# Hi and lo weight parts in one pair tile, placed by how many columns move past them

## The chip, the cores and the metric

The kernel runs on one core of one Trainium2 chip. The metric is the device time of one execution in microseconds (us), lower is better. TensorE is called PE in the profile, its weight loads PEld; VectorE is DVE, ScalarE is ACT, GpSimd is POOL, SyncE is SP.

## The reference

Two decoder layers over one sequence of 512 tokens, 2048 wide, in float32. Each layer is an RMSNorm with a shift, scale and gate made from a conditioning vector, then a mixer, then a residual add; a last RMSNorm follows.

```python
for i in range(DEPTH):                                   # DEPTH = 2
    shift, scale, gate = jnp.split((silu(c) @ ada_w[i] + ada_b[i])[:, None, :], 3, axis=-1)
    h = rmsnorm(x, norm_g[i]) * (1.0 + scale) + shift
    y = retention_branch(...) if i == 0 else mla_branch(...)
    x = x + gate * y
return rmsnorm(x, final_norm_g)
```

`retention_branch` projects `h` (2048) to q, k (8 heads of 256 each), v and a gate (8 heads of 512 each), rotates q and k, runs a causal retention with a decay per head, normalises per head, multiplies with SiLU of the gate and projects 4096 back to 2048. `mla_branch` projects `h` to two latents of 512, a rotary key of 64 and a gate of 2048, expands the latents to 16 heads (192 for q and k, 128 for v), runs causal attention, multiplies with SiLU of the gate and projects 2048 back to 2048.

## The kernel before, in words

*Three matmuls for one product.* A float32 operand is split into a hi part, rounded to the type `float32r`, and a lo part, the rest: ACT writes hi with a copy, DVE writes lo with a subtraction (`split`, L136). A product is then three matmuls into one PSUM bank: hi by hi, hi by lo, lo by hi (`mm3`, L161; the same order by hand at L409, L806 to L808, L905, L1387, L1651 and L2309). Each matmul is preceded by a load of its 128 by 128 stationary operand (LDWEIGHTS), and 256 or 512 columns of the other operand then move through.

*Where weights live.* A weight block of 2 x 512 columns comes by DMA into a `raw` tile (three of them), and its parts go into a tile of tag `whi` and one of tag `wlo`, 4096 bytes per partition each, three of each. `load_w` (L140) does this for the plain projections, `plain_steps` (L738) for the listed steps, `o1_unit` (L1367), `o2_unit` (L2259), `first_load` (L319) and `unit_prepare` (L1870) for their own. `turns` (L782) hands out tiles in turn for the steps with seven products: three out of four times `whi` and `wlo`, the fourth time a tile pair of the open pool (`own_h`, `own_l` in pool `lp`, two tiles `bm` in `l2`). Some units use tiles of other tags instead (`big`, `k4b`).

*Where 512 columns move, and where 256.* In most stages the weight part is stationary and a whole row of 512 tokens moves, or 128 tokens are stationary and 512 weight columns move. Four places have 256 columns moving past stationary weight parts:

- `seven_rows_steps` (L887, its matmul at L905): the q and k projections of heads 2 to 5 and two of the four gate blocks of the second layer (`g2`). A 2 x 2 block product is made from seven half-size products, so half the tokens, 256, move at a time. Its `prepare` (L931) forms the sums on DVE and splits them.
- `ga_half` (L1639, L1651), the first three units of the second layer's first gate block.
- `tail_block` (L1474, L1387), the last four units of the first layer's output projection.
- `o2_end` (L2322, L2309), the last four units of the second layer's.

*Order.* The work is a list of `Step`s: loads run three units ahead on SP's queue, `prepare` one step ahead on DVE and ACT, `multiply` on PE; `behind` and `queued` fix each engine's order as written. Further DVE work goes beside the steps: products for the modulation (L1089), rotations, softmax.

*Layout.* SBUF tiles lie one behind the other in the order in which their tags first appear, in units of 32 bytes, the base pool first and the pools `l0`, `lp`, `l1` and `l2` in turn behind it. An unused tile `spacer` of 32 bytes (L125) and an oversized `qn_s` (L1743) fill it up. By the sum of the sizes `big` begins at byte 6976 of a partition, the `whi` and `wlo` tiles at 147008 and the open pool at 171840; these and all the tiles of 4096 and 2048 bytes between them start 64 bytes past a multiple of 128 (and of 256).

Of the kernel before, what the change touches and what calls it, by code (L numbers as in the profile page):

```python
# [9 lines left out]
F32 = mybir.dt.float32  # L10
# [39 lines left out]
def hybrid_trunk_kernel(  # L50
# [88 lines left out]

    def load_w(parts, a, b, name, later=None, where=None):  # L140

        raw = base.tile([P, a, b], F32, tag="raw", bufs=3, name=f"{name}_raw")
        for dst, src in parts:
            nc.sync.dma_start(dst(raw), src)
        where = where or (("whi", 3), ("wlo", 3))
        hi, lo = (
            base.tile([P, a, b], F32R, tag=tag, bufs=n, name=f"{name}_{p}") for p, (tag, n) in zip(("hi", "lo"), where)
        )
        if later is None:
            split(raw, hi, lo)  # L150
        else:
            later.append(lambda: split(raw, hi, lo))
        return hi, lo
# [165 lines left out]
    def first_load(kind, u):  # L319

        cn = 512
        tags = (("k4b", 4), ("k4b", 4)) if kind == "g" else (("whi", 3), ("wlo", 3))
        raw = big(f"{kind}0_{u}_raw", F32) if u == 0 else base.tile(
            [P, 2, cn], F32, tag="raw", bufs=3, name=f"{kind}0_{u}_raw"
        )
        c0 = {"v": 4096, "g": 8192}.get(kind)
        for dst, src in qk_parts(0, u) if kind == "qk" else [(whole, rows(w_ret_in, u, 2, c0, cn))]:
            nc.sync.dma_start(dst(raw), src)

        def prepare():  # L330
            hl = [base.tile([P, 2, cn], F32R, tag=t, bufs=n, name=f"{kind}0_{u}_{t}{i}") for i, (t, n) in enumerate(tags)]
# [376 lines left out]
    lp = tc.tile_pool(name="lp", bufs=1)  # L708
    lpp = lp.__enter__()

    def keep_rows(ps, dst_d, r0, name, func=AF.Identity, own=None):
# [25 lines left out]

    def plain_steps(nu, kn, parts, cn, name, take, n, lhs, rhs, evac, seeded=False, **kw):  # L738

        banks = {}  # L740

        def step(u):
# [7 lines left out]
            def prepare():  # L750
                w["hl"] = [
                    base.tile([P, kn, cn], F32R, tag=tag, bufs=3, name=f"{name}_{u}_{tag[1]}") for tag in ("whi", "wlo")
                ]
                split(w["raw"], *w["hl"])
# [26 lines left out]

    def turns(raw_tags, part_tags):  # L782
# [8 lines left out]
        def part_tiles(shape, name):  # L791
            n[1] += 1
            pool, tags, bufs = part_tags[n[1] % len(part_tags)]
            return [pool().tile(shape, F32R, tag=tag, bufs=bufs, name=f"{name}_{p}") for p, tag in zip("hl", tags)]

        return raw_tile, part_tiles

    def seven_steps(h, block, form, raw_tile, part_tiles, finish, rows):


        x_, s_, y_, z_, m1, m4, m5 = ([None] * 2 for _ in range(7))
# [13 lines left out]
        def step(second, u):  # L815
# [14 lines left out]
            def prepare():  # L830
                e, o = w["e"], w["o"]
                if not second:
                    eh, el = part_tiles([P, 2, T], f"{n}e")
                    DVE.tensor_sub(e[:, 1, :], e[:, 1, :], e[:, 0, :])
# [3 lines left out]
                    DVE.tensor_sub(el, e, eh.bitcast(F32))  # L838
                    oh, ol = part_tiles([P, 2, T], f"{n}o")
                    ACT.copy(oh, o)  # L840
# [3 lines left out]
                else:  # L844
                    oh, ol = part_tiles([P, 2, T], f"{n}o")
# [3 lines left out]
                    eh, el = part_tiles([P, T], f"{n}e")  # L849
                    ACT.copy(eh, e)  # L850
# [36 lines left out]
    def seven_rows_steps(name, load_half, acts, sums, raw_tile, part_tiles, finish, rows):  # L887
# [30 lines left out]
        def step(second, u):  # L918
# [12 lines left out]
            def prepare():  # L931
                e, o = w["e"], w["o"]
                if not second:
                    e0, e1, o0, o1 = (t[:, :, j * H : (j + 1) * H] for t in (e, o) for j in range(2))
                    eh, el = part_tiles([P, 2, T], f"{n}e")
                    DVE.tensor_sub(e1, e1, e0)
# [3 lines left out]
                    DVE.tensor_sub(el, e, eh.bitcast(F32))  # L940
                    oh, ol = part_tiles([P, 2, T], f"{n}o")
                    ACT.copy(oh, o)
# [3 lines left out]
                else:  # L946
                    oh, ol = part_tiles([P, 2, T], f"{n}o")
# [4 lines left out]
                    eh, el = part_tiles([P, T], f"{n}e")  # L952
                    ACT.copy(eh, e)
# [35 lines left out]
    def heads_steps(h):  # L989
# [24 lines left out]
        ((lambda: lpp, "own_r", 3), (lambda: base, "raw", 3)),  # L1014
        ((lambda: lpp, ("own_h", "own_l"), 1), *3 * ((lambda: base, ("whi", "wlo"), 3),)),
    )
# [141 lines left out]
    def retention(h, own, own2=None):  # L1158
# [207 lines left out]

    def o1_unit(n, r, u, kn, cn, where=(("whi", 3), ("wlo", 3))):  # L1367
# [12 lines left out]
        return w, (load, prepare)  # L1380
# [72 lines left out]
    def second_out():  # L1453
        outs(2, range(4))
        for b in range(4):
# [5 lines left out]
            3, 0, u, 1, 2 * T,  # L1461
            {4: 2 * (("big", 16),), 5: 2 * (("big", 16),), 6: 2 * (("k4b", 4),)}.get(u, (("whi", 3), ("wlo", 3))),
        )
# [155 lines left out]
    rotary2, kr = [], {}  # L1619

    def l2_tile(tag, bufs, name, shape=(P, T), dt=F32):
        return pools["l2"].tile(list(shape), dt, tag=tag, bufs=bufs, name=name)
# [13 lines left out]

    ga = g2_steps(0, seeded=True)

# [103 lines left out]

    qn_s = base.tile([P, 32], F32, name="qn_s")[:, :NT]  # L1743

# [24 lines left out]
    def latent_parts(n, g_c):  # L1769
# [9 lines left out]

    wc = w_mla_in[:, 0:1024].rearrange("k (j n) -> k j n", j=2)  # L1780
    turns2 = turns(
        ((lambda: pools["l2"], "bw", 2), (lambda: base, "raw", 3)),
        ((lambda: pools["l2"], ("bm", "bm"), 2), *3 * ((lambda: base, ("whi", "wlo"), 3),)),
    )
    steps += seven_steps(
# [84 lines left out]
    def unit_prepare(kind, pr, u):  # L1870
        raw = unit_raw.pop((kind, pr, u))
        cn, tags = (384, (("whi", 3), ("wlo", 3))) if kind == "uq" else (512, 2 * (("k4b", 4),))
        hi, lo = unit_parts[kind, pr, u] = [
            base.tile([P, 2, cn], F32R, tag=t, bufs=n, name=f"{kind}_{pr}_{u}_{i}") for i, (t, n) in enumerate(tags)
        ]
        if kind == "ukv":
# [69 lines left out]
    def attend(h):  # L1946
# [13 lines left out]
        def exps(i):  # L1960
            n = (i + 1) * P
            if i == 0:
                side["sm"] = small(f"sm_{h}", NT)
                if s == 0:
                    p_.extend(l2_tile("pp", 5, f"p_{h}_{j}") for j in range(NT))
                else:
                    both = [l2_tile("bm", 2, f"p_{h}_{j}", (P, 2, T)) for j in range(2)]
                    p_.extend(both[j // 2][:, j % 2, :] for j in range(NT))
            DVE.tensor_add(ps[i][:, i * P : n], ps[i][:, i * P : n], mask)
# [187 lines left out]
    for i, step in enumerate(steps):  # L2157
        if i == n_p:
            lp.__exit__(None, None, None)
            l1 = tc.tile_pool(name="l1", bufs=1)  # L2160
            pools["l1"] = l1.__enter__()
        if i == n_l2:
            l1.__exit__(None, None, None)
            l2 = tc.tile_pool(name="l2", bufs=1)
            pools["l2"] = l2.__enter__()
        with behind(S_):
            while n_loaded < min(n_prepared + 3, len(loads)):
# [305 lines left out]
```

## Time and profile before

| | us |
|---|---|
| median of 3 runs | 2149.7 (2149.39 to 2150.03) |
| the profiled execution, its own time | 2149.59 |
| span of that execution, first to last instruction | 2147.8 |
| PE busy in it | 2122.6 |
| DVE busy | 1675.3 |
| ACT busy | 1056.7 |

The granted TensorE clock was 0.998 over the span. "L905" is line 905 of the kernel before. A matmul's recorded duration overlaps with the next one's, so the time that a matmul takes is read from start to start, or from the length of a stretch and the number of matmuls in it.

### The profile page before, as it was taken

What the parts mean: (1) busy time and instruction counts of PE and PEld (TensorE: products, weight loads), DVE (VectorE), ACT (ScalarE), POOL (GpSimd) and SP (SyncE); (2) the same over time, 40 slices, a digit from 0 to 9 for tenths busy, and PEclk for the clock granted to TensorE, in tenths of its full rate; (3) what the DMA queues carried; (4) which work ended last, traced back from release to release, by engine and by line L of the source; (5) the groups of instructions that cost most, each with busy time, mean ns of one, the idle gap of its engine ahead of it and who ended that gap; (6) DMA issues with size and microseconds to landing.
All of it is one profiled execution on the core that took longest, in us unless ns stands there. A gap on an engine that the chain in (4) does not pass through costs nothing.

```text
span 2147.8 us, 30042 instructions
## 1 busy us (share of the span) xinstructions
PE 2122.6 (99%) x11100; PEld 1824.9 (85%) x11100; DVE 1675.3 (78%) x2482; ACT 1056.7 (49%) x1604; POOL 106.5 (5%) x178
## 2 busy tenths in 40 slices
PE   7999999999999999999999999999999999999998
PEld 5887898988889888888888888898889989988887
DVE  7899788888878789766777777668978788886745
ACT  5764444444444444434344544445446565664434
POOL 1000000000000000000000000010001000000000
PEclk9999999999999999999999999999999999999999
DMA  9976687877777778755647566553456644346734
GB/s 381 395 281 197 225 277 229 275 241 259 255 259 259 237 235 283 261 181 185 237 155 246 185 207 240 169 176 115 159 189 203 187 128 147 118 133 221 244 109 137
DMA packets 229782, 462.96 MB, mean 216 GB/s; under 512 B 20817, under 2 KB 84337, under 8 KB 225793
## 3 DMA queue, kind: packets, MB, share of 16 engines
q1 hardware_dynamic: 217424, 421.85, 59.6%
q0 software_dynamic: 11920, 38.91, 4.6%
q8 instruction: 87, 1.43, 0.3%
q14 instruction: 61, 0.50, 0.1%
q10 hardware_dynamic: 290, 0.27, 0.0%
HBM read 417.96 MB, written 43.00 MB: 215 GB/s over the span
## 4 chain that ended last, share of the span: by engine, by line
PE 82%; DVE 7%; DMA 5%; issue 2%; ACT 2%; POOL 1%; SPq 0%; DVEq 0%; POOLq 0%; ACTq 0%
PE o L1387 9%; PE o L2309 4%; PE x L806 2%; PE x L807 2%; PE y L806 2%; PE s L806 2%; PE x L808 2%; PE y L808 2%; PE s L808 2%; PE s L807 2%; PE y L807 2%; PE y_qk L905 2%; PE s_qk L905 2%; PE x_qk L905 2%; DMA mod<-in_ada_t_dram 2%
## 5 line engine op out<-in xcount | busy, mean ns | idle before, releaser
L1387 PE MATMUL o<-o_h,o_whi 128*128 128x512 f32 (+1 forms) x496 | 192.3, 388 | 0.0
L1387 PE MATMUL o<-o_h,o_wlo 128*128 128x512 f32 (+1 forms) x496 | 191.9, 387 | 0.1
L1387 PE MATMUL o<-o_l,o_whi 128*128 128x512 f32 (+1 forms) x496 | 191.3, 386 | 0.0
L1387 PEld LDWEIGHTS o<-o_h,o_wlo 128*128 128x128 f32 x496 | 93.2, 188 | 20.1 <-DVE o_wlo L138 1.5
L138 DVE TENSOR_TENSOR o_wlo<-o_r,o_whi 128x1024 fp32r<-128x1024 f32 x61 | 74.5, 1223 | 44.1 <-ACT o_whi L137 43.5
L1387 PEld LDWEIGHTS o<-o_h,o_whi 128*128 128x128 f32 x496 | 93.2, 188 | 18.2
L1387 PEld LDWEIGHTS o<-o_l,o_whi 128*128 128x128 f32 x496 | 93.2, 188 | 18.2
L165 PE MATMUL qk<-hT,qk_l 128*128 128x512 f32 x192 | 74.8, 390 | 1.5 <-DVE qk_l L138 1.5
L358 DVE SCALAR_TENSOR_TENSOR aw<-aw,c_all 128x2048 f32<-128x2048 f32 (+1 forms) x35 | 73.0, 2101 | 2.7 <-DMA aw<-in_ada_t_dram 2.6
L163 PE MATMUL qk<-hT,qk_h 128*128 128x512 f32 x192 | 75.0, 391 | 0.0
L164 PE MATMUL qk<-hT,qk_h 128*128 128x512 f32 x192 | 74.7, 389 | 0.0
L1089 DVE SCALAR_TENSOR_TENSOR mod<-mod,c_odd 128x1024 f32<-128x1024 f32 x48 | 58.0, 1220 | 20.1 <-DMA mod<-in_ada_t_dram 20.1
L137 ACT CAST o_whi<-o_r 128x1024 fp32r<-128x1024 f32 x61 | 63.4, 1051 | 20.8 <-PE o L1387 18.4
L138 DVE TENSOR_TENSOR o_w_lo<-o_w_raw,o_w_hi 128x1024 fp32r<-128x1024 f32 x32 | 38.9, 1220 | 32.7 <-ACT o_w_hi L137 32.6
L1089 DVE SCALAR_TENSOR_TENSOR mod<-mod,c_bm 128x1024 f32<-128x1024 f32 x48 | 58.5, 1219 | 0.0
L2309 PE MATMUL o<-o_h,o_w_hi 128*128 128x512 f32 (+1 forms) x160 | 55.6, 348 | 0.0
L2309 PE MATMUL o<-o_h,o_w_lo 128*128 128x512 f32 (+1 forms) x160 | 55.5, 347 | 0.0
L2309 PE MATMUL o<-o_l,o_w_hi 128*128 128x512 f32 (+1 forms) x160 | 55.4, 347 | 0.0
L1242 ACT ACTIVATE yn<-y,nmr,gn_r 128x512 f32<-128x512 f32 x32 | 22.3, 778 | 62.0 <-DVE nmr L1236 62.0
L137 ACT CAST o_w_hi<-o_w_raw 128x1024 fp32r<-128x1024 f32 x32 | 33.5, 1050 | 36.3 <-PE o L2309 32.5
L164 PE MATMUL o<-o_l,o_w_hi 128*128 128x512 f32 x128 | 50.1, 391 | 0.5 <-DVE o_l L138 0.5
L137 ACT CAST o_h<-o_in 128x1024 fp32r<-128x1024 f32 x24 | 25.2, 1052 | 51.1 <-PE o L164 47.2
(1608 smaller groups left out, 6893.4 us busy)
## 6 DMA issues: line engine op xcount, KB each, us to landing
mod<-in_ada_t_dram SPq DMA_DIRECT2D x96, 512.0 KB, 5.8
o_r<-in_ret_w_out_dram SPq DMA_DIRECT2D x64, 512.0 KB, 5.3
aw<-in_ada_t_dram SPq DMA_DIRECT2D x30, 1024.0 KB, 9.0
mod_gate<-in_ada_t_dram SPq DMA_DIRECT2D x32, 512.0 KB, 5.0
o_w_raw<-in_mla_w_out_dram SPq DMA_DIRECT2D x32, 512.0 KB, 4.0
qk_r<-in_ret_w_in_dram SPq DMA_DIRECT2D x48, 256.0 KB, 3.2
qk_r<-qk_d SPq DMA_DIRECT2D x32, 256.0 KB, 5.7
v_r<-v_d SPq DMA_DIRECT2D x32, 256.0 KB, 6.2
```

Of the source, the lines that this page charges most:

```text
L137: ACT.copy(hi, src)
L138: DVE.tensor_sub(lo, src, hi.bitcast(F32))
L163: PE.matmul(o, lhs[0], rhs[0], start=first and not seeded, stop=False, skip_group_check=seeded)
L164: PE.matmul(o, lhs[0], rhs[1], start=False, stop=False, skip_group_check=seeded)
L165: return PE.matmul(o, lhs[1], rhs[0], start=False, stop=last, skip_group_check=seeded)
L806: PE.matmul(banks[b], a[0], w[0], start=first, stop=False, skip_group_check=True)
L807: PE.matmul(banks[b], a[0], w[1], start=False, stop=False, skip_group_check=True)
L808: PE.matmul(banks[b], a[1], w[0], start=False, stop=True, skip_group_check=True)
L905: PE.matmul(o, w[wp][:, i, b * P : (b + 1) * P], a[ap], start=first and i + b + k == 0, stop=k == 2, skip_group_check=True,)
L1089: DVE.scalar_tensor_tensor(out=aw, in0=aw, scalar=1.0, in1=silu_c[j], op0=ALU.mult, op1=ALU.mult, accum_out=mc[:, j, b : b + 1],)
L1387: PE.matmul(o, w[i][:, ki, c0 + b * P : c0 + (b + 1) * P], a[j], start=first and i + j == 0, stop=last and i == 1, skip_group_check=True,)
L2309: PE.matmul(banks2[b][:, cols], w[0][i][:, 0, b * P : (b + 1) * P], o2_moving(w, u, cols)[j], start=u + i + j == 0, stop=u == KD - 1 and i ...
```

## The change: what it does

The tags `whi` and `wlo` go. In their place stand three tiles `pair0` to `pair2` of 2 x 1024 + 16 float32 each (8256 bytes, which is 64 more than two parts). A hi and a lo part are views of one pair, 1024 elements apart, beginning at element 16 (`EVEN`) or at element 0 (`ASIDE`). `ASIDE` is given at the four places where 256 columns move past stationary weight parts, as far as their parts lie in pairs: all of `seven_rows_steps`, the first three units of `ga`, unit 7 of the first output projection's tail, the last two units of the second's. All else is `EVEN`. The pools' own parts are pairs likewise (`own`).

Further: the pairs are allocated between the small column tiles at the start of the base pool; `rt` and `mhalf` become one tile, `spacer` goes, `qn_s` shrinks to 64 bytes, the tag `st6` of pool `l1` goes (its four tiles come from `small`), and pool `l1` begins with a `gap` of 64 bytes. The probabilities of every second head (`exps`) lie in the own pair of `l2` instead of two `bm` tiles.

```diff
-    mhalf = base.tile([P, NT], F32, name="mhalf")
+    few = base.tile([P, 2 * NT], F32, name="few")
+    rt, mhalf = few[:, :NT], few[:, NT:]
     DVE.memset(mhalf, -0.5)
-    rt = base.tile([P, 4], F32, name="rt")
-    spacer = base.tile([P, 8], F32, name="spacer")
-    DVE.memset(spacer, 0.0)
...
-    def load_w(parts, a, b, name, later=None, where=None):
+    def load_w(parts, a, b, name, later=None, where=None, halved=False):
...
-        where = where or (("whi", 3), ("wlo", 3))
-        hi, lo = (
-            base.tile([P, a, b], F32R, tag=tag, bufs=n, name=f"{name}_{p}") for p, (tag, n) in zip(("hi", "lo"), where)
-        )
+        hi, lo = two_tiles(where, [P, a, b], name, ASIDE if halved else EVEN)
...
-    a_col = [base.tile([P, KD], F32, name=f"a_col{i}") for i in range(2)]
-    b_col = [base.tile([P, KD], F32, name=f"b_col{i}") for i in range(2)]
-    gate_c = [base.tile([P, KD], F32, name=f"gate_c{i}") for i in range(2)]
+    EVEN, ASIDE = 16, 0
+
+    def pair_tile(pool, tag, name):
+        return pool.tile([P, 2 * 1024 + EVEN], F32R, tag=tag, bufs=1, name=name)
+
+    a_col, b_col, gate_c, ready, n_pairs = [], [], [], {}, [0]
+    for i in range(3):
+        ready[i] = pair_tile(base, f"pair{i}", f"pair_{i}")
+        if i < 2:
+            for cols, name in ((a_col, "a_col"), (b_col, "b_col"), (gate_c, "gate_c")):
+                cols.append(base.tile([P, KD], F32, name=f"{name}{i}"))
+
+    def next_pair(name):
+        i = n_pairs[0] % 3
+        n_pairs[0] += 1
+        return ready.pop(i, None) or pair_tile(base, f"pair{i}", name)
+
+    def parts_of(pair, shape, at):
+
+        n = math.prod(shape[1:])
+        views = [pair[:, 1024 * i + at : 1024 * i + at + n] for i in range(2)]
+        return views if len(shape) == 2 else [v.rearrange("p (k n) -> p k n", k=shape[1]) for v in views]
+
+    def two_tiles(where, shape, name, at=EVEN):
+
+        if where is None:
+            return parts_of(next_pair(name), shape, at)
+        return [base.tile(list(shape), F32R, tag=t, bufs=n, name=f"{name}_{i}") for i, (t, n) in enumerate(where)]
...
     def seven_rows_steps(...)
...
-                    eh, el = part_tiles([P, 2, T], f"{n}e")
+                    eh, el = part_tiles([P, 2, T], f"{n}e", ASIDE)
...
-                st = l1_tile("st6", 4, f"st_{h}_{i}", (P, 6))
+                st = small(f"st_{h}_{i}", 6)
...
-            hl = [base.tile([P, kn, cn], F32R, tag=t, bufs=b, name=f"o1_{n}_{r}_{u}_{t}{i}") for i, (t, b) in enumerate(where)]
+            hl = two_tiles(where, [P, kn, cn], f"o1_{n}_{r}_{u}_p", ASIDE if kn == 1 and u > 3 else EVEN)
...
-    ga = g2_steps(0, seeded=True)
+    ga = g2_steps(0, seeded=True, halved=3)
...
-    qn_s = base.tile([P, 32], F32, name="qn_s")[:, :NT]
+    qn_s = base.tile([P, 16], F32, name="qn_s")[:, :NT]
...
+            l1_tile("gap", 1, "gap", (P, EVEN))
...
-        wt = load_w([(whole, rows(w_mla_out, u, kn, r * T, cn))], kn, cn, f"o2_w{r}_{u}", where=where)
+        halved = kn == 1 and u >= KD - 4
+        wt = load_w([(whole, rows(w_mla_out, u, kn, r * T, cn))], kn, cn, f"o2_w{r}_{u}", where=where, halved=halved)
```

More of the change, by code (lines that the diff above doesn't have):

```diff
@@ L321, in first_load @@
         cn = 512
-        tags = (("k4b", 4), ("k4b", 4)) if kind == "g" else (("whi", 3), ("wlo", 3))
+        where = (("k4b", 4), ("k4b", 4)) if kind == "g" else None
         raw = big(f"{kind}0_{u}_raw", F32) if u == 0 else base.tile(
@@ L330, in prepare @@
         def prepare():
-            hl = [base.tile([P, 2, cn], F32R, tag=t, bufs=n, name=f"{kind}0_{u}_{t}{i}") for i, (t, n) in enumerate(tags)]
+            hl = two_tiles(where, [P, 2, cn], f"{kind}0_{u}_p")
             ACT.copy(hl[0], raw)
@@ L750, in prepare @@
             def prepare():
-                w["hl"] = [
-                    base.tile([P, kn, cn], F32R, tag=tag, bufs=3, name=f"{name}_{u}_{tag[1]}") for tag in ("whi", "wlo")
-                ]
+                w["hl"] = two_tiles(None, [P, kn, cn], f"{name}_{u}_p", ASIDE if u < halved else EVEN)
                 split(w["raw"], *w["hl"])
@@ L780, in halves, with turns @@
         return tuple((t[0][:, j, :], t[1][:, j, :]) for j in range(n))
-    def turns(raw_tags, part_tags):
+    def turns(raw_tags, own):
         n = [0, 0]
@@ L789, in raw_tile, with part_tiles @@
             return pool().tile(shape, F32, tag=tag, bufs=bufs, name=f"{name}_r")
-        def part_tiles(shape, name):
+        def part_tiles(shape, name, at):
             n[1] += 1
-            pool, tags, bufs = part_tags[n[1] % len(part_tags)]
-            return [pool().tile(shape, F32R, tag=tag, bufs=bufs, name=f"{name}_{p}") for p, tag in zip("hl", tags)]
+            return parts_of(next_pair(name) if n[1] % 4 else own(name), shape, at)
         return raw_tile, part_tiles
     def seven_steps(h, block, form, raw_tile, part_tiles, finish, rows):
+        at = EVEN
         x_, s_, y_, z_, m1, m4, m5 = ([None] * 2 for _ in range(7))
@@ L1014, in hybrid_trunk_kernel @@
         ((lambda: lpp, "own_r", 3), (lambda: base, "raw", 3)),
-        ((lambda: lpp, ("own_h", "own_l"), 1), *3 * ((lambda: base, ("whi", "wlo"), 3),)),
+        lambda name: own_ready.pop() if own_ready else pair_tile(lpp, "own", name),
     )
@@ L1619, in hybrid_trunk_kernel, with l2_pair @@
     rotary2, kr = [], {}
+    l2_ready = []
+    def l2_pair(name):
+        return l2_ready.pop() if l2_ready else pair_tile(pools["l2"], "own", name)
     def l2_tile(tag, bufs, name, shape=(P, T), dt=F32):
@@ L1780, in hybrid_trunk_kernel @@
     wc = w_mla_in[:, 0:1024].rearrange("k (j n) -> k j n", j=2)
[L1781 to L1784, printed above, removed]
+    turns2 = turns(((lambda: pools["l2"], "bw", 2), (lambda: base, "raw", 3)), lambda name: l2_pair(name))
     steps += seven_steps(
@@ L1871, in unit_prepare @@
         raw = unit_raw.pop((kind, pr, u))
[L1872 to L1875, printed above, removed]
+        cn, where = (384, None) if kind == "uq" else (512, 2 * (("k4b", 4),))
+        hi, lo = unit_parts[kind, pr, u] = two_tiles(where, [P, 2, cn], f"{kind}_{pr}_{u}_p")
         if kind == "ukv":
@@ L1966, in exps @@
                 else:
-                    both = [l2_tile("bm", 2, f"p_{h}_{j}", (P, 2, T)) for j in range(2)]
-                    p_.extend(both[j // 2][:, j % 2, :] for j in range(NT))
+                    both = l2_pair(f"p_{h}_").bitcast(F32)
+                    p_.extend(both[:, j * T : (j + 1) * T] for j in range(NT))
             DVE.tensor_add(ps[i][:, i * P : n], ps[i][:, i * P : n], mask)
```

22 lines of the change are left out of this document (12 added, 10 removed).

## The prediction

> **What bounds the kernel now.** I read the page first: its busy table, and the shares of the chain of work that ended last.
>
> ```profile
> span 2147.8 us, 30042 instructions
> ...
> PE 2122.6 (99%) x11100; PEld 1824.9 (85%) x11100; DVE 1675.3 (78%) x2482; ACT 1056.7 (49%) x1604; POOL 106.5 (5%) x178
> ...
> PE 82%; DVE 7%; DMA 5%; issue 2%; ACT 2%; POOL 1%; SPq 0%; DVEq 0%; POOLq 0%; ACTq 0%
> ```
>
> PE is busy all the time and carries 82% of the chain, so what counts is how often a matmul starts. PE's busy time can't tell that: a matmul's recorded duration overlaps the next one's. So the second view is the table of busy times by stretch, for stretches that hold one shape alone. Columns: stretch, its length, busy time and instruction count of PE, PEld, DVE, ACT and POOL, granted clock, DMA share, GB/s.
>
> ```profile
> 323.41:399.60 76.19, 76.19 (x339) 63.07 (x337) 63.21 (x79) 35.52 (x42) 3.59 (x7) 1.00 0.75 242
> 283.10:323.41 40.31, 40.31 (x337) 40.31 (x336) 34.88 (x46) 19.00 (x23) 3.58 (x7) 1.00 0.82 274
> 399.60:439.91 40.31, 40.31 (x337) 40.31 (x336) 34.89 (x46) 18.99 (x23) 3.60 (x7) 1.00 0.82 273
> 516.10:556.41 40.31, 40.31 (x337) 40.31 (x336) 34.88 (x46) 19.01 (x23) 3.62 (x7) 1.00 0.82 277
> 632.60:672.91 40.31, 40.31 (x337) 40.31 (x336) 34.89 (x46) 18.99 (x23) 3.98 (x8) 1.00 0.83 275
> 1617.36:1701.47 84.11, 84.11 (x706) 84.11 (x704) 66.48 (x89) 49.29 (x75) 6.23 (x7) 1.00 0.60 181
> 1419.36:1443.83 24.47, 24.37 (x202) 24.03 (x200) 16.10 (x37) 8.59 (x19) 3.45 (x6) 1.00 0.23 72
> 1443.83:1463.12 19.29, 18.70 (x155) 18.33 (x154) 17.54 (x43) 9.68 (x21) 2.33 (x4) 1.00 0.40 136
> 2109.94:2133.84 23.90, 23.90 (x201) 23.90 (x200) 14.13 (x34) 13.38 (x30) 3.44 (x3) 1.00 0.03 12
> ```
>
> The first row is 336 matmuls of 512 columns (L806 to L808; the count has three that reach in over the edge): 76.19 / 336 = 226.8 ns from one start to the next. The next four are the `qk` stages of heads 2 to 5, 336 matmuls of 256 columns each (L905): 40.31 / 336 = 120.0 ns, four times alike, with PE busy for the whole stretch. The fifth L905 stretch is `g2`: 672 of its 706 matmuls are L905's. These are pure rate: no wait stands in them, and the granted clock is 1.00.
>
> Now the arithmetic on which all else rests. 256 more columns cost 226.8 - 120.0 = 106.8 ns, so streaming 256 columns costs 106.8 ns and each matmul pays 120.0 - 106.8 = **13.2 ns on top**, whatever its width. The change can only touch those 13.2 ns, and only for 256 columns.
>
> The third view is the timeline where the width changes from 512 to 256 (start, duration, engine, line, operation):
>
> ```profile
> 1419.13 0.39 PE L1387 MATMUL o<-o_h,o_wlo 128*128 128x512 f32 x1
> 1419.13 0.19 PEld L1387 LDWEIGHTS o<-o_h,o_big 128*128 128x128 f32 x1
> 1419.36 0.28 PE L1387 MATMUL o<-o_h,o_big 128*128 128x256 f32 x1
> 1419.36 0.19 PEld L1387 LDWEIGHTS o<-o_l,o_big 128*128 128x128 f32 x1
> 1419.47 0.28 PE L1387 MATMUL o<-o_l,o_big 128*128 128x256 f32 x1
> 1419.47 0.31 PEld L1387 LDWEIGHTS o<-o_h,o_big 128*128 128x128 f32 x2
> 1419.59 0.40 PE L1387 MATMUL o<-o_h,o_big 128*128 128x256 f32 x2
> 1419.71 0.19 PEld L1387 LDWEIGHTS o<-o_l,o_big 128*128 128x128 f32 x1
> 1419.83 0.28 PE L1387 MATMUL o<-o_l,o_big 128*128 128x256 f32 x1
> ```
>
> A weight load starts together with a matmul and serves the next one. Beside 512 columns it has ended long before it is needed. Beside 256 columns it is just in time: load at 1419.36, its matmul at 1419.47, 0.11 us later; from the second on, 0.12 us. So the same load took one hundredth less the first time, and in steady state something adds to it, or to the matmul beside it. In the steady stretch the record of the load is longer too:
>
> ```profile
> L905 PEld LDWEIGHTS x_qk<-hT,qk_00e_h x32: 188/192/192, 282.9 to 633.7; 128*128 128x128 f32 x32
> L905 PEld LDWEIGHTS s_qk<-sums,qk_00e_h x32: 192/192/192, 284.4 to 635.1; 128*128 128x128 f32 x32
> L1387 PEld LDWEIGHTS o<-o_h,o_wlo 128*128 128x128 f32 x496 | 93.2, 188 | 20.1 <-DVE o_wlo L138 1.5
> ```
>
> 192 ns beside 256 columns against 188 beside 512. Two readers of the same memory, each working all the time, with 13.2 ns of every 120 lost between them: that is where an address could matter.
>
> **The change part by part.** *Addresses.* In the layout before, every tile that a `float32r` matmul reads, moving or stationary, starts 64 bytes past a multiple of 128. Afterwards the sum of the tile sizes puts the three base pairs at bytes 6528, 14976 and 23424, and the own pairs at 171904, all multiples of 128, while `big`, `k4`, `k4b` and `sums` stay at 64 past one. Parts placed at `EVEN` are again 64 past: the 512-column streams see the same offsets as before, and I cost them at nothing. Parts placed at `ASIDE` are now half of 128 bytes apart from what moves beside them. That is the whole of the new behaviour.
>
> *How many.* L905: 4 x 336 + 672 = 2016, all of them. Then three smaller places:
>
> ```profile
> L1651 PE MATMUL g<-h,g_h 128*128 128x256 f32 x96 | 17.5, 284 | 0.4 <-ACT h L1509 0.4
> L1651 PE MATMUL g<-h,g_l 128*128 128x256 f32 x48 | 13.2, 284 | 0.0
> L1387 PE MATMUL o<-o_h,o_whi 128*128 128x256 f32 x16 | 4.5, 283 | 0.0
> L2309 PE MATMUL o<-o_h,o_w_hi 128*128 128x256 f32 x64 | 18.3, 285 | 0.0
> ```
>
> L1651 has 96 + 48 = 144; L1387 has 16 in each of three passes, 48 (its other 256-column units lie in `big` and `k4b` and don't move); L2309 has 3 x 64, of which the units KD-2 and KD-1, half, come from pairs: 96. Together **2304**.
>
> *Price of one.* No row of before has the two operands 64 bytes apart in a 256-column stream, so this is bounded from both sides. Best: the load's own time is then the limit, 0.11 us in the timeline, 110 ns with its rounding: 10 ns less, 2304 x 10 = 23.0 us. Worst: the relation of today is the lucky one and the loss grows by as much as I take it to shrink. I take half of the fixed part, 6.6 ns, to 113.4 ns: the row nearest to "a 256-column matmul without the steady-state loss" is that first pair in the timeline, whose load (0.11) and start behind its neighbour leave it between 0.11 and 0.12. 2304 x 6.6 = **15.2 us less**. At these places PE is the path, so I count all of it.
>
> The TensorE page of the Trainium skill ("TensorE: Matmul & The Clock Gate", section "Wait — 56ns, not 53.3ns?") gives N / 2.4 GHz + about 2.5 ns between warm matmuls; the trace's 13.2 ns fixed part disagrees with those 2.5, and as an estimate from that page the pitch could come down to 109.2 ns, 24.9 us over 2304.
>
> *What must keep up.* DVE writes each lo part and forms the sums. In a `qk` stage it is busy 34.9 of 40.3 us; at 113.4 ns the stage takes 38.1 us, so DVE has 3.2 us left. Its lead is short, though:
>
> ```profile
> 287.07 1.22 DVE L940 TENSOR_TENSOR qk_01e_l<-qk_01e_r,qk_01e_h 128x1024 fp32r<-128x1024 f32 x1
> ...
> L905 PE MATMUL x_qk<-hT,qk_01e_h x8: 283/283/283, 288.9 to 290.1; 128*128 128x256 f32 x8
> ```
>
> The lo part is done at 288.29, and the third matmul of its step, about 288.9 + 0.24 = 289.1, is the first to need it: 0.8 us. A step of 48 matmuls gets 48 x 6.6 = 0.32 us shorter, so the lead shrinks to about half a microsecond and holds. If it did not, this would be the next wait: PE behind DVE's lo part. DMA at 0.82 would go to 0.87.
>
> *One tile for both parts.* Matmuls that read the hi half still wait for ACT alone, as those on `hT`, which has both halves in one tile, do now. A pair comes free when its last reader is done, one matmul (0.12 us) later than the hi tile did; ACT's next cast waits for that, with DVE's subtraction behind it, inside a step of 5.76 us (48 x 120). Nothing. The same pool turns remain: three pairs and one own, for three hi and lo tiles and one own. `st6` among the 24 `small` tiles, the two memsets made one, a shift of 64 bytes for `l0`: nothing that PE waits for. On SP's and POOL's queues nothing is moved.
>
> *Sum.* The profiled execution took 2149.59 us, 1.8 more than its span of 2147.8 and 0.1 under the median of 2149.7. 2149.6 - 15.2 = **2134.4 us**.
>
> **The rivals.**
>
> *The floor (15%).* With the loss gone altogether the load's 0.11 us binds: 2149.6 - 23.0 = 2126.6. For it: the load at 1419.36. Against it: the 512-column stream has its load done in half its time and pays the 13.2 ns just as well, so part of them may be no collision at all, but the exchange of weights.
>
> *Addresses don't matter (16%).* If the 13.2 ns are that exchange, they stay: 2149.6. For it: they are the same at 256 and 512 columns, and the `sums` and `hT` streams, which lie in quite different places, both run at 120.0. Against it: the first 256-column pair is at 0.11. The SBUF page ("SBUF — State Buffer", "Who interferes with whom") says that TensorE has two independent read ports, one for each operand, and that it never waits on anyone; by that rule this is the outcome. The trace's longer load, 192 for 188, speaks against the rule, but does not refute it. Here belongs also that the layout misses its offsets and all streams stay alike.
>
> *The other way (23%).* The place is the same, L905's stream, and the mechanism too: today both readers step through the 128 bytes in the same order, the load at half the matmul's rate. If that is the order in which they meet least, half a turn makes them meet more, and the load, which is just in time, passes the cost on at once. A loss as large as the forecast gain gives 126.6 ns and 2149.6 + 15.2 = 2164.8. It decides from 1.9 ns more per matmul on (4.3 us over 2304). For it: nothing in the trace shows the new relation, and all `float32r` matmuls run in the old one without a single slow stage. Against it: a rate of 120.0 that is already 13.2 over its streaming.
>
> **How the numbers follow.** About 0.2%, 4.3 us, is what can be told from no change here. The forecast, 111 to 118 ns or 2129 to 2145 us, has 46%; with the floor, faster has 61%. No difference has 16%. Slower has 23%. The range goes from 2125, just under the floor, to 2156, which takes in no change and the milder part of the other way; about 2 in 10 are left out, all above. The likeliest case alone would have 2129 to 2145.
>
> **What would show it.** Right: the four `qk` stretches shrink from 40.3 to about 38.1 us with 336 matmuls, `g2` by about 4.4 us, the 512-column stretch stays at 76.2, and PE still has no idle time in them. Floor: 37.0. Wrong: `qk` stretches at 40.3 (addresses don't matter) or 42.5 (the other way); a 512-column rate other than 226.8 (the layout is not what I worked out); or gaps at L905 ended by a DVE lo part (the lead was too short, and the gain goes there).

## The result: faster, by a quarter of what was forecast

| | before | after |
|---|---|---|
| median of 19 runs, us | 2149.66 (2147.5 to 2151.38) | 2145.94 (2143.77 to 2148.81) |
| ratio after to before, 95% interval | | 0.9983 (0.9976 to 0.9990) |
| span of the profiled execution, us | 2147.8 | 2143.2 |

The change gains 3.7 us where 15.2 were forecast. Lines have moved: L905 is now L924, L806 to L808 are L825 to L827, L1387 is L1406, L1651 is L1675, L2309 is L2331. The page of after, its busy table and chain:

```profile
span 2143.2 us, 29960 instructions
...
PE 2115.7 (99%) x11100; PEld 1816.8 (85%) x11100; DVE 1677.3 (78%) x2481; ACT 1054.5 (49%) x1604; POOL 106.6 (5%) x178
...
PE 85%; DVE 5%; DMA 5%; issue 2%; ACT 1%; POOL 1%; SPq 0%; POOLq 0%; DVEq 0%; ACTq 0%
```

PE is as full as before, with the same 11100 matmuls, so the gain is in their rate. Busy times by stretch, in the columns of the prediction; the stretches are the same matmuls as there (its three small places are left out), then two that the argument will need:

```profile
322.41:398.65 76.24, 76.24 (x338) 62.99 (x337) 63.97 (x81) 35.21 (x42) 3.38 (x6) 1.00 0.74 236
282.84:322.41 39.57, 39.57 (x337) 39.57 (x336) 34.15 (x45) 18.90 (x24) 3.79 (x8) 1.00 0.86 288
398.65:438.22 39.57, 39.57 (x337) 39.56 (x336) 34.15 (x45) 18.90 (x24) 4.32 (x9) 1.00 0.89 292
514.54:554.11 39.57, 39.57 (x338) 39.57 (x336) 34.15 (x45) 18.89 (x24) 4.34 (x9) 1.00 0.87 286
630.35:669.92 39.57, 39.57 (x337) 39.57 (x336) 34.15 (x45) 18.89 (x24) 4.69 (x9) 1.00 0.87 291
1614.53:1697.17 82.64, 82.64 (x705) 82.64 (x704) 66.26 (x89) 49.13 (x75) 5.92 (x7) 1.00 0.60 179
1441.53:1445.27 3.74, 3.74 (x36) 3.74 (x35) 3.39 (x9) 2.33 (x6) 1.63 (x3) 1.00 0.88 310
1450.10:1460.18 10.08, 10.08 (x91) 10.08 (x90) 10.08 (x26) 6.18 (x13) 0.00 (x0) 1.00 0.06 24
```

The 512-column stretch is unchanged: 76.24 / 336 = 226.9 ns. Each `qk` stage is 0.74 us shorter, 39.57 / 336 = **117.8 ns** from start to start where 120.0 had been and 113.4 were forecast; `g2` is 1.47 us shorter where 4.4 were forecast. The last two rows are L1675: 33 matmuls in 3.74 us and 89 in 10.08 us, both **113.3 ns**. So the forecast rate exists, in a small place, with the same kind of matmul, and the large place doesn't reach it. Between these two groups lie 13 matmuls of L1675, behind a start-to-start time of 204 ns, that take 117.8 ns each: both rates are already there in this one trace, at one line. The four stages and `g2` make 4 x 0.74 + 1.47 = 4.4 us; the span is 4.6 shorter.

The records carry a mark of it. L924 in after, the first two groups of the first stage (duration in ns, least / median / most; then first and last start in us):

```profile
L924 PEld LDWEIGHTS x_qk<-hT,qk_00e x12: 187/188/188, 282.6 to 284.0; 128*128 128x128 f32 x12
L924 PE MATMUL x_qk<-hT,qk_00e x12: 279/279/280, 282.8 to 284.1; 128*128 128x256 f32 x12
L924 PEld LDWEIGHTS s_qk<-sums,qk_00e x12: 187/188/188, 284.1 to 285.4; 128*128 128x128 f32 x12
L924 PE MATMUL s_qk<-sums,qk_00e x12: 279/279/280, 284.3 to 285.5; 128*128 128x256 f32 x12
```

The loads are back at 188 ns, as beside 512 columns, where before had 192; the matmuls' records are 279 ns where before had 283. Part of the loss is gone, from the first matmul of the stage on, and part stays.

### The profile page after: what moved, and what is told of

It is laid out like the page before. It is cut to its first block, busy times and chain, and to the rows that moved or that the text cites. A ratio compares the mean times of both kernels' runs of the same rounds, so it can differ in the third digit from the quotient of the medians.

```text
span 2143.2 us, 29960 instructions
## 1 busy us (share of the span) xinstructions
PE 2115.7 (99%) x11100; PEld 1816.8 (85%) x11100; DVE 1677.3 (78%) x2481; ACT 1054.5 (49%) x1604; POOL 106.6 (5%) x178
## 4 chain that ended last, share of the span: by engine, by line
PE 85%; DVE 5%; DMA 5%; issue 2%; ACT 1%; POOL 1%; SPq 0%; POOLq 0%; DVEq 0%; ACTq 0%
PE o L1406 11%; PE o L2331 4%; PE s L825 2%; PE x L825 2%; PE x L826 2%; PE y L825 2%; PE s L826 2%; PE y L826 2%; PE s L827 2%; PE x L827 2%; PE y L827 2%; PE s_qk L924 2%; PE x_qk L924 2%; PE y_qk L924 2%; PE qk L160 2%; PE qk L158 2%
## 5 line engine op out<-in xcount | busy, mean ns | idle before, releaser
L1406 PE MATMUL o<-o_h,o_p 128*128 128x512 f32 (+1 forms) x1088 | 323.4, 378 | 0.2 <-DVE o_p L136 0.2
L1406 PEld LDWEIGHTS o<-o_h,o_p 128*128 128x128 f32 x1088 | 199.8, 188 | 38.4 <-DVE o_p L136 1.6
L1406 PE MATMUL o<-o_l,o_p 128*128 128x512 f32 (+1 forms) x544 | 204.8, 377 | 0.0
L1406 PEld LDWEIGHTS o<-o_l,o_p 128*128 128x128 f32 x544 | 102.3, 188 | 18.5
L136 DVE TENSOR_TENSOR o_p<-o_r,o_p 128x1024 fp32r<-128x1024 f32 x64 | 78.1, 1223 | 49.2 <-ACT o_p L135 48.5
L2331 PE MATMUL o<-o_h,o_w 128*128 128x512 f32 (+1 forms) x320 | 82.2, 346 | 0.0
L135 ACT CAST o_p<-o_r 128x1024 fp32r<-128x1024 f32 x64 | 66.5, 1051 | 25.7 <-PE o L1406 18.5
L160 PE MATMUL qk<-hT,qk_p 128*128 128x512 f32 x192 | 74.8, 390 | 1.5 <-DVE qk_p L136 1.5
L158 PE MATMUL qk<-hT,qk_p 128*128 128x512 f32 x192 | 75.0, 391 | 0.0
L159 PE MATMUL qk<-hT,qk_p 128*128 128x512 f32 x192 | 74.7, 389 | 0.0
L2331 PEld LDWEIGHTS o<-o_h,o_w 128*128 128x128 f32 x320 | 55.9, 188 | 7.5
L2331 PE MATMUL o<-o_l,o_w 128*128 128x512 f32 (+1 forms) x160 | 55.2, 345 | 0.0
L158 PE MATMUL o<-o_h,o_w 128*128 128x512 f32 x128 | 50.1, 391 | 0.0
L160 PE MATMUL o<-o_h,o_w 128*128 128x512 f32 x128 | 49.8, 389 | 0.0
```

Source lines behind the costliest of these rows:

```text
L135: ACT.copy(hi, src)
L136: DVE.tensor_sub(lo, src, hi.bitcast(F32))
L158: PE.matmul(o, lhs[0], rhs[0], start=first and not seeded, stop=False, skip_group_check=seeded)
L159: PE.matmul(o, lhs[0], rhs[1], start=False, stop=False, skip_group_check=seeded)
L160: return PE.matmul(o, lhs[1], rhs[0], start=False, stop=last, skip_group_check=seeded)
L1406: PE.matmul(o, w[i][:, ki, c0 + b * P : c0 + (b + 1) * P], a[j], start=first and i + j == 0, stop=last and i == 1, skip_group_check=True,)
```

## The experiments

Before the first four runs I had three explanations for the 117.8: stop flags (the mark on the last matmul of an accumulation), which come at every third matmul at L924; the switch between the two halves of a PSUM bank, the memory that the products are added up in; or something outside L924. A control came with them.

**x1_even**: the new tiles and all the rest of the change, but no part at element 0.

```diff
-    EVEN, ASIDE = 16, 0
+    EVEN, ASIDE = 16, 16
```

> The changed kernel with ASIDE = 16 as EVEN: pairs, pools and allocation stay, only the 64 bytes go. Theory (the 64-byte relation between the moving and the stationary operand sets the pitch): all 256-column stretches return to 120.0 ns a matmul (40.3 us for the 336 of a qk stage), the time to that of before, 2149.7 within 1.5 us. Rival (the gain comes from the other layout: one tile for both parts, weights at low addresses): pitches stay at 117.8 and 113.3 ns, the time at 2146.

Measured: 2150.8 us, ratio 1.0006 (0.9997 to 1.0015). A `qk` stage takes what it took before:

```profile
282.45:322.77 40.32, 40.32 (x338) 40.31 (x337) 34.34 (x45) 18.91 (x24) 3.96 (x9) 1.00 0.86 286
```

The pair tiles, the merged columns and the moved pools gain nothing; all of the gain is the 64 bytes.

**x2_stops**: at L924 one stop flag for 12 matmuls in place of one for 3.

```diff
-  start=first and i + b + k == 0, stop=k == 2,
+  start=first and i + b + k == 0, stop=i + b + k == 4,
```

> The changed kernel; in the seven-row products the stop flag is set on one matmul in twelve (the last of a product) and not on every third. Theory S (a matmul that ends an accumulation group costs the 256-column stream 13.3 ns, which is why L905's successor runs at 117.8 ns and the three other places, almost without stops, at 113.3): 113.3 + 13.3/12 = 114.4 ns, a qk stage in 38.4 us instead of 39.6, the whole 6 to 7 us faster than the changed kernel, 2139. Rival P (the switch between the two halves of a PSUM bank every three matmuls costs it): unchanged, 117.8 ns and 2146.

Measured: 2145.66 us, ratio 0.9986 (0.9977 to 0.9995). The first row is the first `qk` stage, the second the same 89 matmuls of L1675 that took 10.08 us above:

```profile
282.91:322.48 39.57, 39.57 (x337) 39.57 (x336) 34.15 (x45) 18.89 (x24) 3.79 (x8) 1.00 0.86 288
1449.75:1460.23 10.48, 10.48 (x91) 10.48 (x90) 10.48 (x26) 6.18 (x13) 0.00 (x0) 1.00 0.05 18
```

Stop flags fall: L924 is at 39.57 again. The second row is the surprise. Nothing at L1675 was edited and its operands lie where they lay, yet 89 matmuls take 10.48 us, 117.8 ns apiece, for 113.3. **One stream at one set of addresses has two rates**, and what differs in the records just ahead of it is small: three matmuls at 113 to 115 ns for 117 to 119, then one at 182 ns from start to start for 160. It isn't the stop flags: with the operands of this group 64 bytes apart, the 89 run at 113.3 in after and in x8 below, and at 117.8 in x2, x3, x4, x5, x7 and x9. So the question is not what is different about L924's operands.

**x3_order**: the loop over the PSUM halves outside, so that the half changes every 6 matmuls in place of every 3.

```diff
-            for i in range(2):
-                a = moving(n, 2 * u + i)
-                for b in range(2):
+            for b in range(2):
+                for i in range(2):
+                    a = moving(n, 2 * u + i)
```

> The changed kernel; in the seven-row products the loop over the two halves of the PSUM bank is the outer one, so that six matmuls in a row write one half, not three; stop flags stay on every third. Theory S (stop flags): unchanged, 117.8 ns. Rival P (switch of the PSUM half): half as many switches, 113.3 + 2.2 = 115.5 ns, a qk stage in 38.8 us, 4 us faster.

Measured: 2146.84 us, ratio 0.9987 (0.9977 to 0.9997); a `qk` stage 39.57 us, as in after. The halves fall too.

**x4_all_aside**: the parts for 512 columns also at element 0; tile sizes as in after.

```diff
-    EVEN, ASIDE = 16, 0
+    EVEN, ASIDE, SPARE = 0, 0, 16
...
-        return pool.tile([P, 2 * 1024 + EVEN], F32R, ...)
+        return pool.tile([P, 2 * 1024 + SPARE], F32R, ...)
...
```

> The changed kernel with EVEN = 0 as ASIDE, so that the parts beside 512 columns, too, lie 64 bytes from what they meet. Theory (collision between the load and the matmul beside it): the 13.2 ns that a 512-column matmul pays shrink likewise, 226.8 to about 220 ns, and with some 4000 such matmuls the time falls by 25 us or more. Rival (with 512 columns the load has time enough and the 13.2 ns are something else): 226.8 ns and 2146. Third: the new relation is worse for 512 columns, over 226.8 ns, and the time rises.

Measured: 2169.26 us, ratio 1.0093 (1.0080 to 1.0107). The first row is the 512-column stretch, where the weight parts move; the second is 200 matmuls of L1406, where they are stationary (45.33 us in after):

```profile
325.98:404.41 78.43, 78.43 (x339) 62.81 (x337) 64.13 (x81) 35.20 (x42) 3.50 (x7) 1.00 0.73 231
1387.93:1433.71 45.78, 45.78 (x201) 37.56 (x200) 30.11 (x37) 23.01 (x33) 5.46 (x10) 1.00 0.65 208
```

78.43 / 336 = 233.4 ns and 45.78 / 200 = 228.9 ns, for 226.9 and 226.7. With 512 columns the distance of 64 bytes costs, and more where the stationary operand is the one ahead. That is why the change has two places, `EVEN` and `ASIDE`, and the loss that the rival "the other way" put at L924 is found here.

With two rates in one stream the question was what chooses. Call an operand's place within 128 bytes its phase; parts at `EVEN` are in the same phase as what they meet. In after, the first 33 matmuls of L1675 are entered from 256-column matmuls with both operands in the same phase; every stage of L924 is entered from 512-column matmuls. That could be tried.

**x5_entry**: the first even part of each L924 stage, 24 matmuls, back in the same phase.

```diff
-  eh, el = part_tiles([P, 2, T], f"{n}e", ASIDE)
+  eh, el = part_tiles([P, 2, T], f"{n}e", EVEN if u == 0 else ASIDE)
```

> The first even part of each seven-row stage (24 matmuls a stage, 120 in all) is filled 64 bytes further, so that the stage begins with 256-column matmuls whose operands have the same phase; all that follow are as in the changed kernel. Theory 'mode of entry': a stream of 256 columns with opposite phases runs at 113.3 ns or at 117.8 ns apiece, and what came before it decides which; entered from 120.0 ns matmuls of 256 columns (as the three small places are) it runs at 113.3. Then the 1896 others of the stages go from 117.9 to 113.3 ns, -8.6 us, the 120 first ones from 117.9 to 120.0, +0.3 us: a span of about 2135 us for 2143.2, a time of about 2137.5 us. Rival 'mode of place': something that belongs to the stages (strides of the operands, banks, queues beside them) makes 117.8 ns; then only the 120 first ones change, +0.3 us, and the time is 2146.2 us.

Measured: 2142.55 us, ratio 0.9964 (0.9951 to 0.9978). The first `qk` stage in parts: its 24 first matmuls; the 312 that follow; the 512-column stretch behind it; then in `g2` 120 matmuls ahead of a wait and 155 behind it.

```profile
282.60:285.47 2.87, 2.87 (x25) 2.87 (x24) 2.83 (x6) 1.57 (x4) 2.42 (x6) 1.00 1.01 336
285.47:320.83 35.36, 35.36 (x314) 35.36 (x313) 30.93 (x40) 17.26 (x21) 1.00 (x3) 1.00 0.88 295
320.83:397.45 76.62, 76.47 (x338) 62.99 (x337) 64.39 (x81) 35.26 (x42) 3.75 (x6) 1.00 0.75 236
1613.93:1627.54 13.61, 13.61 (x123) 13.61 (x122) 10.97 (x16) 10.62 (x22) 2.74 (x2) 1.00 0.45 135
1632.14:1650.40 18.26, 18.26 (x158) 18.26 (x157) 13.78 (x20) 11.66 (x16) 0.97 (x2) 1.00 0.80 241
```

35.36 / 312 = **113.3 ns**: entered this way, the stage keeps the forecast rate to its end. The same matmuls in after took 36.74 us (285.67 to 322.41). "Mode of entry" holds, "mode of place" falls. In `g2`, 13.61 / 120 = 113.4 up to the wait, 18.26 / 155 = 117.8 behind it: a wait can change the rate. The records show the three states one after another, the same phase at 283 ns, then the fast rate at 276 (after's slow one is 279):

```profile
L924 PEld LDWEIGHTS s_qk<-sums,qk_00e x12: 192/192/192, 283.9 to 285.2; 128*128 128x128 f32 x12
L924 PE MATMUL s_qk<-sums,qk_00e x12: 283/283/283, 284.0 to 285.4; 128*128 128x256 f32 x12
L924 PEld LDWEIGHTS z_qk<-hT,qk_00o x12: 187/188/192, 285.4 to 286.6; 128*128 128x128 f32 x12
L924 PE MATMUL z_qk<-hT,qk_00o x12: 276/276/276, 285.5 to 286.7; 128*128 128x256 f32 x12
```

The span went down 3.8 us, not the 8 expected. The four `qk` stages gained 4 x 1.34 us; `g2` gained only 0.6; the 89 of L1675 took 10.48 us again, 0.40 more than in after; and a `qk` stage that ends sooner finds the next stage less ready. The third row above is 0.38 us longer than in after, and the table of waits names a part of it:

```profile
PE s L825 <- DVE m_qk L1070: 0.5, 3, 0.2
```

That wait (three times, 0.5 us in all) isn't in after.

**x6_aside8**: 32 bytes in place of 64.

```diff
-    EVEN, ASIDE = 16, 0
+    EVEN, ASIDE = 16, 8
```

> The parts whose 256-column matmuls were moved lie 32 bytes from the beginning in place of 0: stationary operand at 32 past a multiple of 128 bytes, moving operand at 64. Theory 'half': it only counts in which 64-byte half of 128 bytes each operand begins; then nothing changes, 117.9 ns in the stages, about 2146 us. Theory 'distance': the gain grows with the distance between the phases; then half of it, 119 ns, about 2148 us. Theory 'alignment': an operand that doesn't begin at a multiple of 64 bytes costs accesses of its own; then over 120 ns and over 2150 us.

Measured: 2144.0 us, ratio 0.9971 (0.9959 to 0.9984).

```profile
282.61:321.81 39.20, 39.20 (x337) 39.20 (x336) 34.05 (x45) 18.93 (x24) 3.67 (x8) 1.00 0.88 289
```

39.20 / 336 = 116.7 ns: none of the three sizes that I had put down. What counts isn't which half of 128 bytes an operand begins in, the gain doesn't halve with the distance, and no second access is paid. Over all 2016 matmuls of L924 it is 116.8 ns, behind the waits as ahead of them, and the first 33 of L1675, entered from the same phase, take 116.7: no second rate showed at this distance.

**x7_even8**: the 512-column parts 32 bytes from the beginning, 256-column ones as in after; tile sizes unchanged.

```diff
-    EVEN, ASIDE = 16, 0
+    EVEN, ASIDE = 8, 0
-  return pool.tile([P, 2 * 1024 + EVEN], F32R, ...)
+  return pool.tile([P, 2 * 1024 + 16], F32R, ...)
...
```

> The other way about: the parts with 512 moving columns (and the rest that stayed 64 bytes in) lie 32 bytes from the beginning, with tile sizes unchanged; the 256-column ones as in the changed kernel. Theory 'half': the 512-column matmuls behave as with no spare bytes at all (229 ns where the part is the stationary operand, 233 where it is the moving one, for 226.7): about 2169 us. Theory 'distance': half of that loss, about 2157 us. Theory 'alignment': a loss of its own, over 2169 us. No effect would be 2146 us.

Measured: 2181.3 us, ratio 1.0143 (1.0125 to 1.0162). The 512-column stretch, and the 200 matmuls of L1406:

```profile
327.58:405.98 78.40, 78.40 (x339) 63.06 (x337) 64.13 (x81) 35.34 (x42) 3.50 (x7) 1.00 0.73 229
1394.08:1440.75 46.67, 46.67 (x202) 37.49 (x201) 30.10 (x37) 23.03 (x33) 5.48 (x10) 1.00 0.64 205
```

78.40 / 336 and 46.67 / 200 are both 233.3 ns. "Half" falls again (it had 229 for L1406). For 512 columns 32 bytes cost as much whichever operand is ahead: about what 64 cost where the stationary one is ahead (233.4), and more than 64 where the moving one is (228.9).

**x8_shift**: 64 bytes ahead of nearly all tiles. To make room two small tiles were dropped, so that the base tiles went 64 bytes up and those of the later pools 64 bytes down: alike in steps of 128, not in steps of 256.

```diff
+    shift = base.tile([P, 16], F32, name="shift")
+    DVE.memset(shift, 0.0)
...
-  gate_sums = [base.tile([P, 2, 8], F32, tag="mod_c", bufs=2, ...) for i in range(2)]
+  gate_sums = [t.rearrange("p (a b) -> p a b", a=2) for t in (a_col[0], b_col[0])]
```

> 64 bytes are put ahead of all tiles but three, so that every operand of a matmul lies 64 bytes further than in the changed kernel: the 256-column ones that were moved have the stationary operand at 64 past a multiple of 128 and the moving one at 0, all others both at 0. Theory 'relative': only the distance between the two operands counts; nothing changes, 117.9 ns in the stages, 226.7 ns for 512 columns, about 2146 us. Theory 'absolute': the gain belongs to a stationary operand at 0; then the 2304 matmuls go back to 120 ns (+5.8 us, about 2152 us) and the others, which now have theirs at 0, change too. Theory 'which one': as with 512 columns, where stationary 64 and moving 0 cost 4.2 ns more than the reverse, it matters which operand is ahead; then 117.9 + 4.2 = 122 ns, +9.7 us, about 2156 us.

Measured: 2148.07 us, ratio 0.9994 (0.9985 to 1.0003). None of the three times came out as put down, because a shift by 64 for some tiles and by -64 for others, 128 bytes between them, had passed for harmless. Two neighbouring groups of six 512-column matmuls, the first with both operands at 0 of 256 bytes, the second with the moving one at 128:

```profile
253.34:254.70 1.36, 1.36 (x7) 1.13 (x6) 1.08 (x3) 1.06 (x1) 0.00 (x0) 1.00 0.98 339
254.70:256.09 1.39, 1.39 (x7) 1.13 (x6) 1.15 (x1) 0.00 (x0) 0.00 (x0) 1.00 0.96 322
```

1.36 / 6 = 226.7 against 1.39 / 6 = 231.7 ns. Joined to their operands' addresses, the 816 matmuls of 512 columns with 128 bytes between the two phases average 232.5 ns from start to start, and the 6306 with none 227.4 (227.1 in after, where all 512-column ones have none; times over 300 ns, behind waits, are left out of both). So a shift of both operands is harmless and the distance between them counts, as "relative" says, but counted in 256 bytes and not in 128. At the `qk` stage (39.03 us) every pair is still 64 bytes apart, in 264 matmuls with the moving operand ahead and in 72 with the stationary one; the groups of the first kind run at 117.8 or at 113.3 ns, so the shift of both left the two rates as they were.

**x9_reentry**: x5 with same-phase parts also behind the three waits in `g2`.

```diff
-  eh, el = part_tiles([P, 2, T], f"{n}e", ASIDE)
+  eh, el = part_tiles([P, 2, T], f"{n}e", EVEN if u == 0 or (u == 3 and name[:2] == "g2") else ASIDE)
...
-  eh, el = part_tiles([P, T], f"{n}e", ASIDE)
+  eh, el = part_tiles([P, T], f"{n}e", EVEN if u == 1 and name[:2] == "g2" else ASIDE)
```

> As x5_entry, and in the two last seven-row stages the even part of the first step after each of the three waits is filled 64 bytes further too (60 to 72 more matmuls at 120 ns). Theory 'mode of entry': the 377 matmuls that ran at 117.9 ns behind the waits of x5_entry run at 113.3 from the second part of their step on, about 300 of them: -1.4 us, the added ones at 120 cost +0.2 to 0.4: a span about 1 us under that of x5_entry (2139.4). Rival: what follows a wait is at 117.9 ns whatever comes first; then +0.2 us.

Measured: **2140.06 us** (2138.96 to 2142.38), ratio 0.9956 (0.9943 to 0.9970): it beats both kernels, after by an interval that doesn't touch its own. Behind the first wait, and behind the third:

```profile
1631.85:1649.49 17.64, 17.64 (x157) 17.64 (x156) 13.69 (x20) 11.54 (x16) 0.91 (x2) 1.00 0.80 242
1679.51:1691.91 12.40, 12.40 (x108) 12.40 (x106) 8.85 (x13) 7.02 (x12) 0.17 (x1) 1.00 0.43 122
```

The span, 2138.3 us, is 1.1 under that of x5, as put down. Behind the first wait, 155 matmuls, the added same-phase ones among them, take 17.64 us for 18.26, and behind the second likewise the fast rate is back. Behind the third it isn't (12.40 / 105 = 118.1). There the same-phase part stands second in its step, so that the stream enters it from the slow rate, and its records show what is different:

```profile
L924 PEld LDWEIGHTS y_g<-sums,g_11e x12: 188/188/190, 1680.6 to 1681.9; 128*128 128x128 f32 x12
L924 PE MATMUL y_g<-sums,g_11e x12: 280/283/287, 1680.7 to 1682.0; 128*128 128x256 f32 x12
L924 PE MATMUL s_g<-sums,g_11o x12: 279/279/280, 1682.1 to 1683.4; 128*128 128x256 f32 x12
```

Loads of 188 to 190 ns, not 192: the same-phase stream didn't reach the steady state that it has elsewhere, and what followed stayed slow. It isn't having been through the same phase that goes with the fast rate, but leaving it with a load of 192.

The small places bear this out. In the eight traces with 64 bytes (after, x2 to x5, x7 to x9), joined to the addresses, 266 groups of two or more matmuls 64 bytes apart, the moving operand ahead, come straight behind same-phase ones of 256 columns. Where the load of the group's first matmul took 192 or 193 ns, the group ran at 113.0 to 113.5 ns, in 235 of 235; where it took 188 to 190, at 115.5 to 118.5, in 31 of 31. All 30 groups entered straight from 512 columns ran at 117.8.

**x10_aside12**: 16 bytes between the phases (`ASIDE = 12`).

> The moved parts lie 48 bytes from the beginning: stationary operand at 48, moving at 64 past a multiple of 128, 16 bytes apart. Equal phases gave 120.0 ns, 64 apart 117.9 or 113.3, 32 apart 116.8. Theory 'any difference': once the phases differ the two reads fall apart, 116 to 118 ns, about 2144 to 2146 us. Theory 'distance': it falls off with the distance, 118.5 to 119.5 ns, 2147 to 2149 us. Theory 'alignment': an operand across a 32-byte border costs accesses of its own: over 120 ns, over 2150 us.

Measured: 2145.85 us, ratio 0.9983 (0.9973 to 0.9993).

```profile
282.67:322.09 39.42, 39.42 (x338) 39.42 (x336) 34.10 (x45) 18.95 (x24) 3.76 (x8) 1.00 0.87 290
```

39.42 / 336 = 117.3 ns: "any difference". But the stages aren't all. The last part of `g2`, behind a wait, and the first 33 matmuls of L1675, entered from the same phase:

```profile
1684.60:1697.07 12.47, 12.47 (x107) 12.47 (x106) 8.85 (x13) 7.03 (x12) 0.18 (x1) 1.00 0.41 119
1441.14:1445.10 3.96, 3.96 (x36) 3.96 (x34) 3.37 (x9) 2.55 (x6) 1.62 (x3) 1.00 0.87 312
```

12.47 / 104 = 119.9 and 3.96 / 33 = 120.0 ns: with 16 bytes there are two rates too, 117.3 and hardly any gain at all, and the entry that gave the fast rate at 64 bytes gives the slow one here. Entered from 512 columns, the three distances take away 2.2 to 3.3 ns; only 64 bytes with the right entry give 6.7.

## Why the prediction was right in sign and wrong in size

- **What bounds the kernel, and the two terms of a matmul's time**: right that PE bounds it. PE has no gap in the `qk` stages, in `g2` and in the 512-column stretch, before or after, and the gain there is in the start-to-start time. That the fixed part is the same for both widths was an assumption: 256 columns gave up half of theirs, 512 columns none.
- **Addresses**: right. 512 columns keep 226.9 ns, all of the gain goes with the 64 bytes (x1: 1.0006), and the 2304 matmuls are those that got faster.
- **Price of one**: this is the step that failed. It took half of the fixed part, 6.6 ns, for all 2304. The 2016 of L924 got 120.0 - 117.8 = 2.2 ns, which is 4.4 us for 13.3. At L1675, 33 matmuls and then 89 got 6.7 ns, and after x5's entry the `qk` stages do too. The size 6.6 was that of one of two rates, and I took the rate to be a property of the addresses alone. That it comes so near to 6.7 is luck: half was a choice between two bounds. The row on which the step leaned, the first pair behind the width's change (0.11 us in the timeline), was read as a sight of the rate without loss. It is an entry, and how a stream is entered is just what keeps L924 from that rate: in after, the first two starts of a `qk` stage are already 0.12 us apart.
- **What must keep up**: right for after; no wait on a DVE lo part stands in the `qk` stretches, and DVE is busy 34.2 of 39.6 us. At the fast rate of x5 a wait of DVE's does come, but at the end of the stage (L825 on `m_qk`), not at the lo part that I had named.
- **One tile for both parts**: right within the spread (x1). One small price shows, in the waits behind the `qk` stages, before and after:

```profile
PE s L163 <- ACT yn L1242: 1.0, 4, 0.3
PE s L158 <- ACT yn L1261: 1.6, 4, 0.4
```

x1, without the 64 bytes, has 1.5 there, so this half microsecond belongs to the rest of the change.

- **Sum**: with 2.2 ns at L924 the same sum gives 2016 x 2.2 = 4.4 us. The small places add 0.8 at L1675 (0.2 and 0.6 for its two long groups) and 0.6 at L2309, now L2331. That makes 5.8, without the 48 of L1406, for a span that fell 4.6; 0.9 of the difference arises between the last `qk` stage and L1406, where the work took 698.4 us for 697.5, and the wait above is most of it. The median fell 3.7; single runs of one kernel lie up to 5.0 us apart.
- **The rivals**: "addresses don't matter" falls. With it falls, for this kernel, the Trainium skill's rule ("SBUF — State Buffer", "Who interferes with whom") that TensorE's two read ports are independent and that it never waits on anyone: with only addresses changed, 256 columns went from 120.0 to 117.8 and 113.3 ns, 512 columns from 226.9 to 233.3. The floor wasn't reached: no steady stream of 256 columns here went under 113. "The other way" was wrong for its place, but its mechanism is real for 512 columns, where every distance that was tried costs 2 to 6.5 ns.

Left open: what in the hardware makes two stable rates out of one set of addresses. The runs show that they exist, that the rate changes at entries and behind waits (and once, in x8, between two parts where the phases of both operands change), and one entry that leads to the fast one; they don't show the cause, nor what decides behind a wait. Whether 32 bytes have a second rate under an entry that this kernel doesn't have isn't known.

## What to carry to other kernels

Where PE is full and a load is only just in time, compare start-to-start times with what the width explains: a constant rest in every matmul can depend on the distance between the two operands' addresses, which costs little to change. Try it for each width by itself, since what helps 256 columns here hurts 512. And before a rate seen at one place is multiplied by a count, see whether the same instruction at the same addresses runs at that rate twice: a stream can have more than one, kept from its entry on.

## What the runs showed of the hardware that I had not expected

- One stream of 256-column `float32r` matmuls, 64 bytes apart in phase, runs at 113.3 or at 117.8 ns apiece and holds either for hundreds of matmuls (312 and 336 here), until a wait or another shape comes between. Entered from 512 columns it was slow each time (30 of 30 entries in six traces); entered from the same-phase stream with a load of 192 ns it was fast each time (235 of 235).
- At 16 bytes the two rates are 117.3 and 119.9, and the entry from the same phase gives the slow one.
- At 512 columns, where the load takes 188 of 227 ns and has long ended, the distance still counts, and the same phase is best: 226.9 ns with none, 228.9 or 233.4 with 64 bytes, 233.3 with 32, 232.5 with 128. So it isn't only a matter of a load that comes just in time.
- The phases are to be counted in 256 bytes at least: operands 128 bytes apart are not the same as operands in one phase.
